# Queries and keys of heads 1 to 4 by seven products of halves with 256 moving columns, and head 5's first

## The chip, the cores and the metric

The kernel runs on one core of one Trainium2 chip. The metric is device time in microseconds (us), lower is better. The core has a matrix engine (TensorE, PE in the profile), a vector engine (DVE), a scalar engine (ACT), GpSimd (POOL) and a queue that issues loads (SyncE, SP).

## The reference, cut to what matters

A trunk of two layers over 512 tokens with 2048 features. The first layer is a retention layer of 8 heads; each has 256 columns of queries, 256 of keys, 512 of values and 512 of gates.

```
h = rmsnorm(x, norm_g[0]) * (1.0 + scale) + shift        # (512, 2048)
proj = h @ w_in                                          # w_in: (2048, 12288)
q, k, v, g = split(proj, [2048, 4096, 8192])
y = chunkwise_retention(rope(q), rope(k) * 256**-0.5, v) # per head
x = x + gate * ((silu(g) * groupnorm(y)) @ w_out)
```

The second layer (latent attention, 16 heads) works on the result. `shift`, `scale` and `gate` come from `silu(c) @ ada_w[i] + ada_b[i]`. The change touches `proj` of the first layer: columns of q and k.

## The kernel before

**Three products.** Every f32 factor is split in two `fp32r` parts, a high one (ACT casts, `L137`) and a low one (DVE subtracts the high part from the value, `L138`). A product is three matmuls into one PSUM bank: high by high, high by low, low by high (`mm3`, `L163` to `L165`). `hT[kt]` is h so split: 16 tiles of 128 features x 512 tokens.

**Steps.** The projections are a list `steps`. A step has units (`load` of weights on SP's queue into a raw tile, `prepare`: high and low part), `multiply` (24 matmuls as a rule) and `follow` (what is done with finished banks). The loop at the end of the printed code goes through them: it issues loads until three units beyond the prepared ones are on their way, prepares the units of step i + 1, multiplies step i, then does the modulation adds fetched in the step before (`rows`: one row is a load of 512 KB and a DVE instruction with an accumulator, `L913`, "mod"; they form the next modulations from `ada_w`), the sums of h if the step has them, and `follow`. `behind` and `queued` tie what is issued to the last instruction of the engines named, so that the blocks stand on their engines' queues in this order; inside of a block a scheduler orders. A queue is worked in order.

**Queries and keys** (`qk_steps`, a head's columns are 512: q and k). Eight steps of two feature blocks; the weights are stationary (128 x 128), h moves with all 512 tokens; four PSUM banks (`acc`). ACT copies the banks out (`keep_rows`, `L641`) and POOL stores them to `qk_d`.

**Values and gates** (`seven_steps`) of one head form a product of 2 x 2 halves with seven products for eight: halves of the tokens, of the features (odd and even blocks), and of the columns (values, gates). DVE forms sums of the weights' halves (`L786` to `L800`); sums of the halves of h lie ready in `sums1` (`form_sums`, 8 pieces u, each two feature blocks). A head is two sweeps of eight steps: the first with four products (24 matmuls of 512 columns a step), the second with three (18). Banks are called x, s, z, y; m1, m4, m5 are copies of them. At the end (`finish`) ACT copies x (values) and applies silu to s, DVE forms `m4` and `m5` (`L850`, `L852`), ACT applies silu to m5 (`L853`), POOL stores. In the names, `vg3_01e` is head 3, first sweep, unit 1, even block; `_r`, `_h`, `_l` are raw tile, high and low part.

**Order before:** q/k of head 1 and 2 (`form_sums` spread over their steps), values/gates of 1 and 2, then q/k and values/gates of 3, of 4 and of 5, then values/gates of 6 and 7; q/k of heads 6 and 7 follow in the next phase, the retention itself from about 960 us on. Head 0 is done ahead of this list.

**Buffers.** Raw tiles: two tags of three each, in turns. Parts: four sets in turns (`own` one, `whi`/`wlo` three). PSUM: `acc` 4 banks and `aux` 4. In the second layer the product `uv` has 256 moving columns.

## Time and profile before

| | |
|---|---|
| median of 3 runs | 2178.03 us (2175.65 to 2179.16) |
| profiled execution | 2178.51 us, span 2176.7 us, granted clock 0.998 |
| PE | 2150.4 us busy, 99% of the span, 10206 matmuls |
| weight loads (PEld) | 1798.4 us, 83% |
| DVE / ACT / POOL | 1563.9 us (72%) / 1015.1 us (47%) / 100.4 us (5%) |
| DMA | 440.26 MB, mean 202 GB/s |

One core, one program: a row of the timeline is start, duration, engine, line, operation, output<-inputs, with a bracket [idle time before it <- what ended it]. A row of groups by line has a count, then busy time and mean ns, then idle time before and what ended it. PE's idle time is what counts where PE is busy 99% of the span.

### The profile page before, as it was taken

Reading aid. Unit: us, or ns where it says so; the run is one execution under the profiler, and the core shown is the slowest. Engines: PE = TensorE matmul, PEld = TensorE weight load, DVE = VectorE, ACT = ScalarE, POOL = GpSimd, SP = SyncE. Lnnn points to the kernel's source line nnn. Section 1 sums busy time; section 2 is a strip of 40 time slices with the busy share of each in tenths; the row PEclk is TensorE's granted clock in tenths of the full one; section 3 lists DMA queues with packets and bytes.
Section 4 is the critical chain, followed back from the end, with each engine's and each line's share of the span. In section 5 each row is a group of like instructions: output and inputs, shape, how many; then the busy total and the mean of one; then the engine's idle time right before and its main releaser. Section 6 shows DMA issues by size and latency. Waiting matters only on the chain.

```text
span 2176.7 us, 27707 instructions
## 1 busy us (share of the span) xinstructions
PE 2150.4 (99%) x10206; PEld 1798.4 (83%) x10206; DVE 1563.9 (72%) x2311; ACT 1015.1 (47%) x1549; POOL 100.4 (5%) x175
## 2 busy tenths in 40 slices
PE   8999999999999999999999999999999999999997
PEld 6888888888888877888888888898888889888887
DVE  8987878676776789656776777667977677775545
ACT  6763344344343454434344445344444365664443
POOL 0000000000000000000000000010000000000000
PEclk9999999999999999999999999999999999999999
DMA  9966767857667778564646465453458723335333
GB/s 387 377 243 199 244 225 231 293 181 268 217 234 251 238 232 296 192 218 152 234 157 220 151 216 185 146 174 107 160 188 314 247 88 100 89 109 183 111 101 133
DMA packets 204971, 440.26 MB, mean 202 GB/s; under 512 B 19313, under 2 KB 56209, under 8 KB 200993
## 3 DMA queue, kind: packets, MB, share of 16 engines
q1 hardware_dynamic: 192768, 399.57, 55.4%
q0 software_dynamic: 11920, 38.91, 4.6%
q8 instruction: 80, 1.31, 0.2%
q14 instruction: 57, 0.47, 0.1%
q10 hardware_dynamic: 146, 0.01, 0.0%
HBM read 395.42 MB, written 43.00 MB: 201 GB/s over the span
## 4 chain that ended last, share of the span: by engine, by line
PE 85%; DVE 7%; issue 4%; ACT 3%; DMA 1%; POOL 0%; DVEq 0%; POOLq 0%; ACTq 0%; SPq 0%
PE o L1211 13%; PE qk L163 4%; PE qk L165 4%; PE qk L164 4%; PE o L2073 4%; PE x L759 2%; PE y L759 2%; PE y L760 2%; PE y L758 2%; PE x L760 2%; PE s L759 2%; PE s L760 2%; PE x L758 2%; PE s L758 2%; PE o L164 2%
## 5 line engine op out<-in xcount | busy, mean ns | idle before, releaser
L1211 PE MATMUL o<-o_h,o_whi 128*128 128x512 f32 (+1 forms) x496 | 192.2, 388 | 0.0
L1211 PE MATMUL o<-o_h,o_wlo 128*128 128x512 f32 (+1 forms) x496 | 191.4, 386 | 0.0
L1211 PE MATMUL o<-o_l,o_whi 128*128 128x512 f32 (+1 forms) x496 | 191.3, 386 | 0.0
L163 PE MATMUL qk<-hT,qk_h 128*128 128x512 f32 x448 | 174.6, 390 | 1.0 <-ACT qk_st L641 1.0
L164 PE MATMUL qk<-hT,qk_h 128*128 128x512 f32 x448 | 174.4, 389 | 0.0
L165 PE MATMUL qk<-hT,qk_l 128*128 128x512 f32 x448 | 174.2, 389 | 0.0
L138 DVE TENSOR_TENSOR o_wlo<-o_r,o_whi 128x1024 fp32r<-128x1024 f32 x61 | 74.6, 1223 | 80.1 <-ACT o_whi L137 80.1
L138 DVE TENSOR_TENSOR qk_l<-qk_r,qk_h 128x1024 fp32r<-128x1024 f32 x56 | 68.1, 1224 | 71.0 <-ACT qk_h L137 70.8
L1211 PEld LDWEIGHTS o<-o_h,o_wlo 128*128 128x128 f32 x496 | 93.2, 188 | 18.7
L1211 PEld LDWEIGHTS o<-o_l,o_whi 128*128 128x128 f32 x496 | 93.2, 188 | 18.3
L1211 PEld LDWEIGHTS o<-o_h,o_whi 128*128 128x128 f32 x496 | 93.2, 188 | 18.3
L163 PEld LDWEIGHTS qk<-hT,qk_h 128*128 128x128 f32 x448 | 84.1, 188 | 18.8 <-ACT qk_st L641 1.5
L165 PEld LDWEIGHTS qk<-hT,qk_l 128*128 128x128 f32 x448 | 84.1, 188 | 17.5
L164 PEld LDWEIGHTS qk<-hT,qk_h 128*128 128x128 f32 x448 | 84.1, 188 | 17.5
L163 PE MATMUL g<-h,g_h 128*128 128x512 f32 x232 | 90.6, 390 | 0.3 <-ACT g_h L137 0.3
L164 PE MATMUL g<-h,g_h 128*128 128x512 f32 x232 | 90.3, 389 | 0.0
L165 PE MATMUL g<-h,g_l 128*128 128x512 f32 x232 | 89.8, 389 | 0.0
L913 DVE SCALAR_TENSOR_TENSOR mod<-mod,c_bm 128x1024 f32<-128x1024 f32 x64 | 78.1, 1220 | 15.3 <-DMA mod<-in_ada_t_dram 15.3
L137 ACT CAST qk_h<-qk_r 128x1024 fp32r<-128x1024 f32 x56 | 57.8, 1052 | 65.7 <-PE qk L164 54.3
L137 ACT CAST o_whi<-o_r 128x1024 fp32r<-128x1024 f32 x61 | 63.5, 1053 | 19.5 <-issue 10.0
L353 DVE SCALAR_TENSOR_TENSOR aw<-aw,c_all 128x2048 f32<-128x2048 f32 x30 | 67.5, 2286 | 0.0
L138 DVE TENSOR_TENSOR o_w_lo<-o_w_raw,o_w_hi 128x1024 fp32r<-128x1024 f32 x32 | 39.0, 1221 | 37.4 <-ACT o_w_hi L137 37.4
(1264 smaller groups left out, 5995.3 us busy)
## 6 DMA issues: line engine op xcount, KB each, us to landing
mod<-in_ada_t_dram SPq DMA_DIRECT2D x128, 512.0 KB, 5.9
o_r<-in_ret_w_out_dram SPq DMA_DIRECT2D x64, 512.0 KB, 4.2
aw<-in_ada_t_dram SPq DMA_DIRECT2D x30, 1024.0 KB, 7.6
qk_r<-in_ret_w_in_dram SPq DMA_DIRECT2D x112, 256.0 KB, 3.9
g_r<-in_mla_w_in_dram SPq DMA_DIRECT2D x32, 512.0 KB, 4.3
o_w_raw<-in_mla_w_out_dram SPq DMA_DIRECT2D x32, 512.0 KB, 3.7
qk_d<-qk_st POOLq DMA_DIRECT2D x32, 256.0 KB, 3.4
qk_r<-qk_d SPq DMA_DIRECT2D x32, 256.0 KB, 6.1
```

The costliest lines, as they stand in the source:

```text
L137: ACT.copy(hi, src)
L138: DVE.tensor_sub(lo, src, hi.bitcast(F32))
L163: PE.matmul(o, lhs[0], rhs[0], start=first and not seeded, stop=False, skip_group_check=seeded)
L164: PE.matmul(o, lhs[0], rhs[1], start=False, stop=False, skip_group_check=seeded)
L165: return PE.matmul(o, lhs[1], rhs[0], start=False, stop=last, skip_group_check=seeded)
L353: DVE.scalar_tensor_tensor(out=aw, in0=aw, scalar=1.0, in1=c_all, op0=ALU.mult, op1=ALU.mult, accum_out=col,)
L758: PE.matmul(banks[b], a[0], w[0], start=first, stop=False, skip_group_check=True)
L759: PE.matmul(banks[b], a[0], w[1], start=False, stop=False, skip_group_check=True)
L760: PE.matmul(banks[b], a[1], w[0], start=False, stop=True, skip_group_check=True)
L913: DVE.scalar_tensor_tensor(out=aw, in0=aw, scalar=1.0, in1=silu_c[j], op0=ALU.mult, op1=ALU.mult, accum_out=mc[:, j, b : b + 1],)
L1211: PE.matmul(o, w[i][:, ki, c0 + b * P : c0 + (b + 1) * P], a[j], start=first and i + j == 0, stop=last and i == 1, skip_group_check=True,)
L2073: PE.matmul(banks2[b][:, cols], w[0][i][:, 0, b * P : (b + 1) * P], o2_moving(w, u, cols)[j], start=u + i + j == 0, stop=u == KD - 1 and i ...
```

## The change

Q and k of heads 1 to 4 are now formed by seven products too (`narrow_steps`), in another division: halves of the columns (q and k, 256 each), of the features (even and odd blocks) and of the tokens (256 each). The sums of the weights' halves are stationary, the halves (or sums) of h move with 256 tokens. All seven banks `m1` to `m7` are held through the one sweep of 14 steps of 24 matmuls with 256 columns. Per quarter of the features a unit `b11` (four blocks of q), and twice a group of `o` (odd blocks of q and k), `a` (even block of k, then three sums on DVE in place) and `b` (no load; what is left in o's raw tile). The banks are joined by ACT copies and eight DVE adds (`after_o`, `after_a`, `after_b`), and stored by four POOL DMAs (`keep`).

Q and k of head 5 come first, plain, with one piece of the sums of h in each of its eight steps; whole h is formed again on ACT (`again`) and not added from its parts on DVE. The order is then q/k and values/gates of 1, of 2, of 3, of 4, then values/gates of 5, 6 and 7. The modulation rows leave the q/k steps in part: steps 0, 2, 3, 6 of a narrow head have one each, and seven of the eight steps of every second sweep (before: four in heads 1 to 4). Step 11 of a narrow head looks two units ahead with loads, not three.

```diff
@@ -653,17 +653,27 @@
             return base.tile(shape, F32R, tag="k4b", bufs=4, name=f"sums_{n}")
         return more(shape, f"sums_{n}")
-    def form_sums(u, acts, sums, staged, more):
+    def sum_slot(n, more):
+        return sums_tile((n - 8) % KD, more)
+    def again(f, kt):
+        k1 = slice(kt, kt + 1)
+        ACT.activation(f, xT[kt // 2][:, kt % 2, :], AF.Identity, bias=b_col[0][:, k1], scale=a_col[0][:, k1])
+    def added(f, kt):
+        DVE.tensor_add(f, h2[kt][:, 0, :].bitcast(F32), h2[kt][:, 1, :].bitcast(F32))
+    def form_sums(u, whole_h, sums, staged, more, slot):
         e, o = (tmp(f"h_{2 * u + i}_f") for i in range(2))
         for f, kt in ((e, 2 * u), (o, 2 * u + 1)):
-            DVE.tensor_add(f, acts[kt][:, 0, :].bitcast(F32), acts[kt][:, 1, :].bitcast(F32))
+            whole_h(f, kt)
...
-            s = sums[2 * u + i] = sums_tile(2 * u + i, more)
+            s = sums[2 * u + i] = slot(2 * u + i, more)
             split(f[i], s[:, :, 0, :], s[:, :, 1, :])
...
-    wvg = w_ret_in[:, 4096:12288].rearrange("k (j n) -> k j n", j=2)
+    def form_half(acts, sums, n, u):
+        if isinstance(n, tuple):
+            kt, half = n
+            return tuple(acts[2 * u + kt][:, a, half * H : (half + 1) * H] for a in range(2))
+        s = sums[2 * u + (n - 1) // 2]
+        return tuple(s[:, (n - 1) % 2, a, :] for a in range(2))
...
-            self.rows, self.sums = rows, sums
+            self.rows, self.sums, self.ahead = rows, sums, 3
             self.beside = {"load": [], "form": [], "multiply": []}
...
@@ -836,6 +852,125 @@
+    def narrow_steps(name, half_of, form, raw_tile, part_tiles, keep):
+        m = [None] * 8
+        put = {}
+        def bank(i):
+            m[i] = (aux if i in (1, 5, 7) else acc)(f"{name}_m{i}")
+        def product(i, n, u, w, first):
+            f = form(n, u)
+            for b in range(2):
+                o, (hi, lo) = m[i][:, b * H : (b + 1) * H], (a[:, b * P : (b + 1) * P] for a in w)
+                for k, (p, q) in enumerate(((hi, f[0]), (hi, f[1]), (lo, f[0]))):
+                    PE.matmul(o, p, q, start=first and b + k == 0, stop=k == 2, skip_group_check=True)
+        def parts(src, shape, n):
+            hi, lo = part_tiles(shape, n)
+            ACT.copy(hi, src)
+            return (hi, lo), lambda: DVE.tensor_sub(lo, src, hi.bitcast(F32))
+        def quarter(g):
+            b11 = {}
+            def step(load, prepare, forms, u0, nu, follow=None):
+                w = {}
+                def ready():
+                    w["p"] = prepare()
+                def multiply():
+                    for i, n, j in forms:
+                        if u0 == 0:
+                            bank(i)
+                        for u in range(nu):
+                            product(i, n, u0 + u, tuple(t[:, u, :] if j is None else t[:, j, u, :] for t in w["p"]), u0 + u == 0)
+                return Step(load, ready, multiply, follow)
...
+            res = [step(load_b11, prepare_b11, [(1, (0, 0), None)], 4 * g, 4)]
+            for s in range(2):
+                res += pair(g, s, step, b11)
+            return res
+        def pair(g, s, step, b11):
+            u0, t, shape = 4 * g + 2 * s, {}, [P, 2, 2, H]
+            last = u0 == KD // 2 - 2
...
+            def prepare_a():
+                a, o, b = t["a"], t["o"], b11["r"][:, 2 * s : 2 * s + 2]
+                DVE.tensor_sub(o[:, 1], o[:, 1], a[:, 0])
+                DVE.tensor_sub(a[:, 0], a[:, 0], b)
+                DVE.tensor_add(a[:, 1], o[:, 1], b)
+                hl, low = parts(a, shape, f"{name}_a{u0}")
+                DVE.tensor_sub(o[:, 0], o[:, 0], a[:, 1])
+                low()
+                return hl
...
+            def after_o():
+                put["1"] = tmp(f"{name}_p1")
+                ACT.copy(put["1"], m[1])
+                c11 = tmp(f"{name}_c11")
+                DVE.tensor_add(c11, m[2], put["1"])
+                keep(0, 0, c11)
+            def after_a():
+                p1, p5, v = put["1"], tmp(f"{name}_p5"), tmp(f"{name}_v")
+                ACT.copy(p5, m[5])
+                DVE.tensor_add(p1, m[6], p1)
+                DVE.tensor_add(v, p1, p5)
+                DVE.tensor_add(v, m[3], v)
+                keep(0, 1, v)
+                put["5"] = p5
+            def after_b():
+                p1, p5 = put["1"], put["5"]
+                DVE.tensor_add(p1, m[7], p1)
+                DVE.tensor_add(p5, p1, p5)
+                keep(1, 1, p5)
+                DVE.tensor_add(p1, m[4], p1)
+                keep(1, 0, p1)
+            return [
+                step(load_o, prepare_o, [(2, (1, 0), 0), (3, 4, 1)], u0, 2, after_o if last else None),
+                step(load_a, prepare_a, [(5, 1, 0), (6, 2, 1)], u0, 2, after_a if last else None),
+                step(lambda: None, prepare_b, [(7, 3, 1), (4, (1, 1), 0)], u0, 2, after_b if last else None),
+            ]
+        return quarter(0) + quarter(1)
...
-            lambda second, u: int(second and (u % 2 == 1 or (h > 4 and u > 0))),
+            lambda second, u: int(second and u > 0),
         )
     sums1, sums2 = {}, {}
@@ -885,11 +1020,33 @@
...
-    steps = qk_steps(1, sums=lambda u: {1: 0, 2: 1, 4: 2, 5: 3, 6: 4}.get(u))
-    steps += qk_steps(2, rows=lambda u: 1, sums=lambda u: {0: 5, 2: 6, 4: 7}.get(u))
+    def narrow_qk(h):
...
+        def keep(half, j, c):
+            r0 = (4 * h + 2 * j) * P
+            POOL.dma_start(
+                qk_d[r0 : r0 + 2 * P, half * H : (half + 1) * H].rearrange("(b p) t -> p b t", p=P),
+                c.rearrange("p (b t) -> p b t", b=2),
+            )
+        return narrow_steps(
+            f"qk{h}", lambda e, j, u0, n: qk_w[j][e][:, u0 : u0 + n, :], lambda n, u: form_half(hT, sums1, n, u),
+            *turns1, keep,
+        )
+    steps = qk_steps(5, sums=lambda u: u)
     for h in range(1, RH):
-        if 2 < h < 6:
-            steps += qk_steps(h, rows=lambda u: 1)
+        if h < 5:
+            block = narrow_qk(h)
+            for i in (0, 2, 3, 6):
+                block[i].rows = 1
+            block[11].ahead = 2
+            steps += block
         steps += heads_steps(h)
@@ -1550,7 +1707,7 @@
         return l2_tile("pt", 4, name, shape, F32R)
     for u, step in enumerate((ga[5], ga[7], g1[0], g1[2], g1[3], g1[5], g1[6], g1[7])):
-        step.beside["form"].append(lambda u=u: form_sums(u, h2, sums2, staged2, more2))
+        step.beside["form"].append(lambda u=u: form_sums(u, added, sums2, staged2, more2, sums_tile))
     latent = {}
@@ -1940,7 +2097,7 @@
             l2 = tc.tile_pool(name="l2", bufs=1)
             pools["l2"] = l2.__enter__()
         with behind(S_):
-            while n_loaded < min(n_prepared + 3, len(loads)):
+            while n_loaded < min(n_prepared + step.ahead, len(loads)):
                 loads[n_loaded]()
                 n_loaded += 1
             if i in (n_p, n_l2):
@@ -1964,7 +2121,7 @@
                 add()
             fetched = []
             if step.sums is not None:
-                form_sums(step.sums, hT, sums1, staged1, more1)
+                form_sums(step.sums, again, sums1, staged1, more1, sum_slot)
         if i + 1 < len(steps):
             for _ in range(steps[i + 1].rows):
                 with behind(S_):
```

On ACT, at the change from a head's gates to the next q/k. Before (gates of head 2, q/k of head 3; `qk3_0`, `qk3_1` are the first units, `v2_st`, `g2_st` the evictions, `m5` the silu of the last gates):

```order
L137 CAST qk3_0_h_3274<-qk3_0_r_3208 128x1024
L641 ACTIVATE v2_st0_3303<-x2_0_2726 128x512
L641 ACTIVATE v2_st1_3306<-x2_1_2727 128x512
L641 ACTIVATE g2_st0_3309<-s2_0_2728 128x512
L641 ACTIVATE g2_st1_3312<-s2_1_2729 128x512
L853 ACTIVATE m5_2_0_3035<-m5_2_0_3035 128x512
L853 ACTIVATE m5_2_1_3037<-m5_2_1_3037 128x512
L137 CAST qk3_1_h_3328<-qk3_1_r_3239 128x1024
L137 CAST qk3_2_h_3366<-qk3_2_r_3271 128x1024
```

After (gates of head 1, q/k of head 2; `b11`, `o0`, `a0`, `b0` are the first four steps' units):

```order
L872 CAST qk2_b11_0_h_2843<-qk2_b11_0_r_2776 128x1024
L641 ACTIVATE v1_st0_2868<-x1_0_2288 128x512
L641 ACTIVATE v1_st1_2871<-x1_1_2289 128x512
L641 ACTIVATE g1_st0_2874<-s1_0_2290 128x512
L641 ACTIVATE g1_st1_2877<-s1_1_2291 128x512
L988 ACTIVATE m5_1_0_2597<-m5_1_0_2597 128x512
L988 ACTIVATE m5_1_1_2599<-m5_1_1_2599 128x512
L872 CAST qk2_o0_h_2890<-qk2_o0_r_2808 128x1024
L872 CAST qk2_a0_h_2926<-qk2_a0_r_2841 128x1024
L872 CAST qk2_b0_h_2961<-qk2_o0_r_2808 128x1024
```

The cast of the second unit stands behind the same eviction and silu as before, and the third and fourth unit's behind it; the fourth casts from o's raw tile.

On DVE, at the same place. Before:

```order
L850 TENSOR_TENSOR m4_2_0_3074<-m4_2_0_3074,y2_0_2732 128x512
L852 TENSOR_TENSOR m5_2_0_3035<-m5_2_0_3035,y2_0_2732 128x512
L850 TENSOR_TENSOR m4_2_1_3076<-m4_2_1_3076,y2_1_2733 128x512
L852 TENSOR_TENSOR m5_2_1_3037<-m5_2_1_3037,y2_1_2733 128x512
L138 TENSOR_TENSOR qk3_1_l_3329<-qk3_1_r_3239,qk3_1_h_3328 128x1024
L913 SCALAR_TENSOR_TENSOR mod_0_2_1_00_3301,mod_0_2_1_c_3300<-mod_0_2_1_00_3301,c_bm0_1733 128x1024
L138 TENSOR_TENSOR qk3_2_l_3367<-qk3_2_r_3271,qk3_2_h_3366 128x1024
L913 SCALAR_TENSOR_TENSOR mod_0_2_1_01_3361,mod_0_2_1_c_3300<-mod_0_2_1_01_3361,c_bm1_1734 128x1024
L138 TENSOR_TENSOR qk3_3_l_3401<-qk3_3_r_3325,qk3_3_h_3400 128x1024
```

After:

```order
L985 TENSOR_TENSOR m4_1_0_2636<-m4_1_0_2636,y1_0_2294 128x512
L987 TENSOR_TENSOR m5_1_0_2597<-m5_1_0_2597,y1_0_2294 128x512
L985 TENSOR_TENSOR m4_1_1_2638<-m4_1_1_2638,y1_1_2295 128x512
L987 TENSOR_TENSOR m5_1_1_2599<-m5_1_1_2599,y1_1_2295 128x512
L873 TENSOR_TENSOR qk2_o0_l_2891<-qk2_o0_r_2808,qk2_o0_h_2890 128x1024
L1070 SCALAR_TENSOR_TENSOR mod_0_2_0_51_2866,mod_0_2_0_c_1780<-mod_0_2_0_51_2866,c_bm1_1777 128x1024
L929 TENSOR_TENSOR qk2_o0_r_2808<-qk2_o0_r_2808,qk2_a0_r_2841 128x512
L930 TENSOR_TENSOR qk2_a0_r_2841<-qk2_a0_r_2841,qk2_b11_0_r_2776 128x512
L931 TENSOR_TENSOR qk2_a0_r_2841<-qk2_o0_r_2808,qk2_b11_0_r_2776 128x512
L933 TENSOR_TENSOR qk2_o0_r_2808<-qk2_o0_r_2808,qk2_a0_r_2841 128x512
L873 TENSOR_TENSOR qk2_a0_l_2927<-qk2_a0_r_2841,qk2_a0_h_2926 128x1024
L873 TENSOR_TENSOR qk2_b0_l_2962<-qk2_o0_r_2808,qk2_b0_h_2961 128x1024
```

Between the low parts of the second and the third unit stand now four sums (`L929` to `L933`) as well as the modulation add.

On DVE, from q/k to the first sweep of values and gates. Before (end of q/k of head 3; the banks are emptied by ACT):

```order
L138 TENSOR_TENSOR qk3_7_l_3539<-qk3_7_r_3465,qk3_7_h_3538 128x1024
L913 SCALAR_TENSOR_TENSOR mod_0_2_1_30_3532,mod_0_2_1_c_3300<-mod_0_2_1_30_3532,c_bm0_1733 128x1024
L786 TENSOR_TENSOR vg3_00e_r_3499<-vg3_00e_r_3499 128x512
L788 TENSOR_TENSOR vg3_00o_r_3500<-vg3_00o_r_3500,vg3_00e_r_3499 128x512
L789 TENSOR_TENSOR vg3_00o_r_3500<-vg3_00o_r_3500 128x512
L790 TENSOR_TENSOR vg3_00e_l_3574<-vg3_00e_r_3499,vg3_00e_h_3573 128x1024
L793 TENSOR_TENSOR vg3_00o_l_3581<-vg3_00o_r_3500,vg3_00o_h_3580 128x1024
L913 SCALAR_TENSOR_TENSOR mod_0_2_1_31_3567,mod_0_2_1_c_3300<-mod_0_2_1_31_3567,c_bm1_1734 128x1024
L786 TENSOR_TENSOR vg3_01e_r_3534<-vg3_01e_r_3534 128x512
```

After (end of q/k of head 2; `c11`, `v`, `p1`, `p5` are what is stored):

```order
L946 TENSOR_TENSOR qk2_c11_3278<-qk2_m2_2931,qk2_p1_3276 128x512
L873 TENSOR_TENSOR qk2_b6_l_3290<-qk2_o6_r_3151,qk2_b6_h_3289 128x1024
L952 TENSOR_TENSOR qk2_p1_3276<-qk2_m6_2978,qk2_p1_3276 128x512
L953 TENSOR_TENSOR qk2_v_3318<-qk2_p1_3276,qk2_p5_3317 128x512
L954 TENSOR_TENSOR qk2_v_3318<-qk2_m3_2944,qk2_v_3318 128x512
L802 TENSOR_TENSOR vg2_00e_r_3281<-vg2_00e_r_3281 128x512
L804 TENSOR_TENSOR vg2_00o_r_3282<-vg2_00o_r_3282,vg2_00e_r_3281 128x512
L805 TENSOR_TENSOR vg2_00o_r_3282<-vg2_00o_r_3282 128x512
L806 TENSOR_TENSOR vg2_00e_l_3329<-vg2_00e_r_3281,vg2_00e_h_3328 128x1024
L809 TENSOR_TENSOR vg2_00o_l_3336<-vg2_00o_r_3282,vg2_00o_h_3335 128x1024
L960 TENSOR_TENSOR qk2_p1_3276<-qk2_m7_2998,qk2_p1_3276 128x512
L961 TENSOR_TENSOR qk2_p5_3317<-qk2_p1_3276,qk2_p5_3317 128x512
```

The adds from the banks m6 and m3 stand ahead of the first unit of values and gates (`vg2_00`), those from m7 and m4 behind it and ahead of `vg2_01`.

On PE, the first matmuls of the second step at the first place. Before (second unit of q/k of head 3; `L163` to `L165` are the three products):

```order
L163 MATMUL qk3_0_3332<-hT_2_388,qk3_1_h_3328 128x512
L164 MATMUL qk3_0_3332<-hT_2_388,qk3_1_h_3328 128x512
L165 MATMUL qk3_0_3332<-hT_2_388,qk3_1_l_3329 128x512
L163 MATMUL qk3_1_3333<-hT_2_388,qk3_1_h_3328 128x512
L164 MATMUL qk3_1_3333<-hT_2_388,qk3_1_h_3328 128x512
L165 MATMUL qk3_1_3333<-hT_2_388,qk3_1_l_3329 128x512
L163 MATMUL qk3_2_3334<-hT_2_388,qk3_1_h_3328 128x512
```

After (step `o0` of head 2):

```order
L868 MATMUL qk2_m2_2931<-hT_1_318,qk2_o0_h_2890 128x256 x2
L868 MATMUL qk2_m3_2944<-sums_9_1453,qk2_o0_h_2890 128x256 x2
L868 MATMUL qk2_m2_2931<-hT_1_318,qk2_o0_l_2891 128x256
L868 MATMUL qk2_m2_2931<-hT_1_318,qk2_o0_h_2890 128x256 x2
L868 MATMUL qk2_m2_2931<-hT_1_318,qk2_o0_l_2891 128x256
L868 MATMUL qk2_m2_2931<-hT_3_403,qk2_o0_h_2890 128x256 x2
L868 MATMUL qk2_m2_2931<-hT_3_403,qk2_o0_l_2891 128x256
L868 MATMUL qk2_m2_2931<-hT_3_403,qk2_o0_h_2890 128x256 x2
```

The weights' part is the stationary tile in both. Ahead of the first matmul with the low part (`o0_l`) stand four with the high one, for two banks, where two for one bank stood before.

## The prediction

> **What bounds the kernel now.** First the page's parts 1 and 4, then the waits of PE, then stretches of the stage that is changed.

> ```profile
> PE 2150.4 (99%) x10206; PEld 1798.4 (83%) x10206; DVE 1563.9 (72%) x2311; ACT 1015.1 (47%) x1549; POOL 100.4 (5%) x175
> PE 85%; DVE 7%; issue 4%; ACT 3%; DMA 1%; POOL 0%; DVEq 0%; POOLq 0%; ACTq 0%; SPq 0%
> ...
> PE qk L163 <- ACT qk_st L641: 1.0, 1, 1.0
> PE x L759 <- DVE vg_01e_l L790: 1.0, 2, 0.5
> PE x L759 <- DVE vg_17o_l L800: 0.6, 1, 0.6
> ```

> TensorE (PE) is the bound: the three waits are all that it waits from 160 to 900 us. Fewer PE cycles there come out as time, and so does every new wait of PE. The stretches (us, then busy time of PE, weight loads, DVE, ACT, POOL, the granted clock, DMA share, GB/s) are q and k of head 3, the first and second sweep of its values and gates, the second sweep of head 5, head 6's two, and the second sweep of head 7:

> ```profile
> 402.49:446.06 43.57, 43.57 (x194) 36.04 (x192) 26.00 (x35) 12.33 (x14) 3.77 (x8) 1.00 0.84 284
> 446.06:490.11 44.05, 44.05 (x194) 36.06 (x192) 33.72 (x40) 19.73 (x22) 0.81 (x2) 1.00 0.65 204
> 490.11:523.24 33.13, 33.13 (x145) 27.03 (x144) 23.41 (x32) 15.42 (x21) 1.91 (x4) 1.00 0.66 213
> 731.61:765.57 33.96, 33.40 (x145) 26.95 (x144) 28.00 (x39) 15.01 (x21) 0.13 (x1) 1.00 0.83 281
> 765.57:810.75 45.18, 44.66 (x194) 35.91 (x193) 39.49 (x49) 21.67 (x26) 4.17 (x8) 1.00 0.76 243
> 810.75:844.19 33.44, 33.39 (x145) 26.96 (x144) 28.00 (x39) 14.99 (x21) 0.13 (x1) 1.00 0.85 284
> ...
> 889.42:922.56 33.14, 33.14 (x146) 27.04 (x145) 21.46 (x30) 15.42 (x21) 1.93 (x4) 1.00 0.56 178
> ```

> q and k of one head are 192 matmuls with 512 columns in 43.57 us: one each 0.2269 us.

> **The matmuls.** Four heads go from 192 such matmuls to 7×8×2×3 = 336 with 256 columns and a new weight block each. The same shape runs today in the second layer; its first and last of 30 in a row, with its weight load:

> ```profile
> 1806.08 0.28 PE L164 MATMUL uv<-ukv,kvT 128*128 128x256 f32 x1
> ...
> 1809.55 0.28 PE L163 MATMUL uv<-ukv,kvT 128*128 128x256 f32 x1
> ...
> L164 PEld LDWEIGHTS uv<-ukv,kvT x128: 187/192/192, 1744.4 to 1970.2; 128*128 128x128 f32 x128
> ```

> 3.47 us over 29 steps is 0.1197 us. A narrow head is 336×0.1197 = 40.2 us, 3.35 less than 43.57; four heads give back 13.4 us. The ends of this price are half of the wide one (0.1135 us, 21.7 us back) and the row itself; I take the row. [...]

> **The start of a narrow head.** A step was 24 wide matmuls, 5.44 us; it is 24 narrow ones, 2.87 us. What ACT and DVE must do between two steps does not halve. The same place in the run before is the change from head 2's gates to head 3's q and k (PE crosses at E = 402.49):

> ```profile
> 402.61 0.68 DVE L852 TENSOR_TENSOR m<-m,y 128x512 f32<-128x512 f32 x1
> 403.21 0.68 DVE L850 TENSOR_TENSOR m<-m,y 128x512 f32<-128x512 f32 x1
> 403.80 0.68 DVE L852 TENSOR_TENSOR m<-m,y 128x512 f32<-128x512 f32 x1
> 406.12 1.23 DVE L138 TENSOR_TENSOR qk_l<-qk_r,qk_h 128x1024 fp32r<-128x1024 f32 x1 [1.64 <-ACT qk_h L137]
> 407.26 1.22 DVE L913 SCALAR_TENSOR_TENSOR mod<-mod,c_bm 128x1024 f32<-128x1024 f32 x1
> 408.41 0.08 DVE L913 DVE_READ_ACCUMULATOR mod<-mod,c_bm 128x1 f32 x1
> ...
> 404.52 0.63 ACT L853 ACTIVATE m<-m 128x512 f32<-128x512 f32 x1 [0.56 <-DVE m L852]
> 405.06 1.98 ACT L137 CAST qk_h<-qk_r 128x1024 fp32r<-128x1024 f32 x2
> ...
> L137 ACT CAST qk_h<-qk_r 128x1024 fp32r<-128x1024 f32 x56 | 57.8, 1052 | 65.7 <-PE qk L164 54.3
> ```

> The second unit's high part is cast behind the last gate's silu, from E+2.57 to E+3.6, and its low part ends at 407.35, E+4.86. Before, PE needed them at E+5.44. Now the same places in the queues hold qk_o, and PE needs it at E+2.87. In the order PE does four matmuls of the high part first (0.48): it starts at 3.65, waits for the low part until 4.90, has 20 left (2.39) and ends the step at 7.30 instead of 5.74. Late: 1.6.

> The next step is dearer. DVE does, behind qk_o's low part, a modulation add (1.15 by the rows), then three dependent subtractions; ACT casts; DVE forms the low part. Subtractions of this size and the form with an accumulator bank:

> ```profile
> 444.72 0.69 DVE L788 TENSOR_TENSOR vg_01o_r<-vg_01o_r,vg_01e_r 128x512 f32<-128x512 f32 x1
> 445.45 0.69 DVE L789 TENSOR_TENSOR vg_01o_r<-vg_01o_r 128x512 f32<-128x512 f32 x1
> 447.82 1.23 DVE L790 TENSOR_TENSOR vg_01e_l<-vg_01e_r,vg_01e_h 128x1024 fp32r<-128x1024 f32 x1 [1.68 <-ACT vg_01e_h L787]
> ...
> 446.26 0.60 ACT L641 ACTIVATE qk_st<-qk 128x512 f32<-128x512 f32 x1 [0.76 <-PE qk L165]
> 446.75 1.04 ACT L787 CAST vg_01e_h<-vg_01e_r 128x1024 fp32r<-128x1024 f32 x1
> ...
> L826 DVE TENSOR_TENSOR y<-y,m 128x512 f32<-128x512 f32 x14 | 9.7, 700 | 5.2 <-PE y L760 5.2
> ```

> A dependent subtraction starts 0.73 after the one before, a free one 0.60 (402.61 to 403.80). So: add E+4.77 to 5.92, subtractions at 5.92, 6.64, 7.24, cast 7.97 to 9.02, low part to 10.27. PE ends that step at 10.32 + 2.39 = 12.71 instead of 8.61: 4.1 late in all. The second pair repeats it with DVE still behind: low part at 19.1, PE wants it at 18.9, 4.3 in all. From there a quarter (seven steps) is 20.1 us for PE, and for DVE seven low parts of 1.14, eight subtractions of 0.66, two modulation adds of 1.15 and two waits of 0.5 for a cast, 16.6, so the rest is in time.

> Head 1 comes behind q and k of head 5, without gates to finish: by the fence above its cast can run at E+0.69 (446.75 against E = 446.06), the low part ends at E+3.0 and costs nothing; the subtraction step ends at 8.45 + 2.39 = 10.84, 2.2 late, 2.5 with the second pair. Sum at the starts: 3×4.3 + 2.5 = 15.4 us. Unseen here is whether the subtractions' operands land; loads are issued three units ahead and q/k loads land in 3.9 us, so I set that at nothing (ends: nothing, and the 1.9 us that a late load cost once, below).

> ```profile
> qk_r<-in_ret_w_in_dram SPq DMA_DIRECT2D x112, 256.0 KB, 3.9
> ```

> **The end of a narrow head.** The banks are now emptied by DVE. Its queue holds three adds that wait for the last matmul of step 13 (F; visible 0.2 later, as 446.26 against 446.06), and behind them the first unit of values and gates: adds at F+0.2, 0.92, 1.64 (0.70 each), subtraction 2.26, cast 2.98 to 4.03, low part to 5.53, second cast to 5.48, its low part to 6.67, then three more adds to 8.62. PE arrives at F+2.87, gets the first high part at 4.08, the second at 5.53, does six and eight matmuls to 8.93, finds the bank of s_1 free, ends at 10.30 instead of 8.31. The next unit's cast ends at 10.31 and its second at 11.76: 0.6 more. So 2.6 us a head, 10.4 in all. Before, ACT emptied these banks, and the stretch 446.06:490.11 is only 0.5 over its 192 matmuls. The ends of this term: 0.1 if the high parts were ready at F+2.87, 4.0 if PE had to take the matmuls in the plain order, each low part behind its high one.

> **Small terms.** Second sweeps of heads 1 to 4 take seven modulation adds instead of four: 33.96, 33.44 and 33.14 with seven against 33.13 with four, 0.4 each, 1.5 in all. Head 5's first sweep now follows head 4's second: 45.18 against 44.05, 1.1. All sums of h in one block of eight steps: per step ACT has a cast 1.0, two activations of 0.80 as below, a wait of 1.3 for three small DVE operations, two casts of 0.6, 5.1 of 5.44 us; only the first is late, behind the eight evictions of head 0, 0.4 (ends 0 and 2).

> ```profile
> L247 ACT ACTIVATE h_2f<-x,b_col,a_col x1: 801/801/801, 44.0 to 44.0; 128x512 f32<-128x512 f32 x1
> ...
> 169.92 0.42 DVE L661 TENSOR_TENSOR sums_f<-h_f 128x256 f32<-128x256 f32 x1
> ...
> L137 ACT CAST sums<-sums_f x4: 616/618/620, 170.8 to 177.1; 128x512 fp32r<-128x512 f32 x4
> ```

> Nothing for the rest: the same 4 MB of weights a head in 14 issues for 16; four stores a head as before, read only after 960 us; 16 adds less on DVE, 16 activations more on ACT, under PE's block.

> **Sum.** −13.4 + 15.4 + 10.4 + 1.5 + 1.1 + 0.4 = +15.4. The profiled run's own time is 2178.5 (span 2176.7), 0.5 above the median of the runs; it gives 2193.9, and I say 2194.

> **Rivals.**
> *Faster.* DVE and ACT run ahead, so the subtraction steps and the first units of values and gates are there in time; only the 1.6 behind the gates' silu stays, at three heads. 2178.5 − 13.4 + 4.7 + 1.5 = 2171. For it: four sets of parts let them prepare three units ahead, and DVE has 3.5 us free in each quarter. Against: their queues are in order, and the rows at 404.52 and 405.06 show the cast stuck behind the silu. It decides when all waits of a narrow head stay under 2.4 us.
> *Even.* The chains are half as long, the waits 13 us: 2181.
> *A late modulation load on top.* With seven adds a sweep DVE has stood still for a load:

> ```profile
> 759.10 1.23 DVE L913 SCALAR_TENSOR_TENSOR mod<-mod,c_bm 128x1024 f32<-128x1024 f32 x1 [1.87 <-DMA mod<-in_ada_t_dram]
> ```

> Once or twice at each of the four starts, in a chain with no slack: 7 to 15 us more, 2201 to 2209. Against: in the new order the loads stand farther ahead.
> *Weight loads show.* If a load could not run under the matmul before it, a narrow matmul would cost its 0.188 us or more: 4×(63.2 − 43.6) = 78 us, 2257. The uv rows at 0.12 us with a load of 0.19 each speak against it. [...]

> **How the numbers follow.** About 0.2% (4.4 us) is what a measurement of this kernel tells from no change. Forecast, 2186 to 2204: 0.58. Late loads: 0.14. Faster: 0.17. Even: 0.09. Weight loads: 0.01; something else 0.01. A range of 2174 to 2207 takes in the even case and the upper edge of the faster one; it leaves out most of the faster one, 0.14, the upper part of the late one, 0.04, and the last two. Faster by over 0.2% 0.17, within 0.07 (most of the even case), slower 0.76.

> **What would show it.** PE of narrow heads spaced at 0.12; 2 to 5 us of PE waits for qk_o_l and qk_a_l at the start of heads 2 to 4, less at head 1; waits for vg_00e, vg_00o and vg_01 behind each narrow head; DVE idle for PE at the three adds. I am wrong if PE passes these places without a wait, or if a narrow head takes under 42 us.

## The result, and the profile after

The changed kernel took 2198.64 us (median of 4, 2196.72 to 2201.54) against 2178.55: slower by 20.1 us, ratio 1.0096 with a 95% interval of 1.0079 to 1.0113. The forecast was 2194, in a range of 2174 to 2207. The profiled execution is the longest of the four, 2201.54 us, its span 23.1 us longer than before.

From the page, the busy times:

```profile
PE 2152.1 (98%) x10782; PEld 1821.0 (83%) x10782; DVE 1641.4 (75%) x2411; ACT 1043.8 (47%) x1581; POOL 103.9 (5%) x175
```

The longest waits of PE from 160 to 1000 us (sum, times, longest):

```profile
PE qk_m L868 <- ACT qk_a_h L872: 5.9, 4, 1.5
PE x L774 <- ACT vg_00e_h L803: 4.6, 4, 1.1
PE qk_m L868 <- DVE qk_a_l L873: 2.1, 4, 0.5
PE z L774 <- ACT vg_00o_h L808: 2.0, 4, 0.5
PE qk_m L868 <- ACT qk_o_h L872: 1.9, 3, 0.6
PE qk_m L868 <- DVE qk_o_l L873: 1.6, 3, 0.5
PE x L775 <- DVE vg_01e_l L806: 1.5, 3, 0.5
```

The waits stand where the prediction put them: qk_o at three heads, qk_a at four, vg_00 behind all four. The stretches (length, then busy time of PE, weight loads, DVE, ACT, POOL, the granted clock, DMA share, GB/s) are q/k of head 1, its two sweeps, the same three of head 2, and the first sweep of head 3:

```profile
204.20:249.45 45.25, 42.32 (x338) 41.71 (x336) 34.90 (x44) 15.63 (x17) 2.27 (x4) 0.96 0.52 162
249.45:295.31 45.86, 45.02 (x192) 35.92 (x193) 40.17 (x48) 20.37 (x22) 1.43 (x2) 1.00 0.66 209
295.31:328.38 33.07, 33.07 (x145) 27.03 (x144) 26.70 (x38) 15.22 (x21) 1.53 (x3) 1.00 0.81 270
328.38:375.64 47.26, 42.90 (x338) 41.88 (x336) 36.90 (x48) 16.31 (x18) 4.24 (x8) 0.96 0.62 199
375.64:421.63 45.99, 45.17 (x192) 35.90 (x193) 40.24 (x48) 20.39 (x22) 1.43 (x2) 1.00 0.65 207
421.63:454.74 33.11, 33.11 (x145) 27.03 (x144) 27.17 (x40) 15.32 (x21) 1.65 (x3) 1.00 0.82 272
501.89:548.42 46.53, 46.03 (x193) 37.29 (x193) 40.18 (x48) 20.36 (x22) 1.44 (x2) 0.96 0.66 206
```

A narrow head is 45.3 to 47.3 us, where the plain one was 43.57. Its stretch ends with PE's first matmul of values and gates and so holds the 1.3 us gap ahead of that matmul as well. What the prediction did not have is in the column of the clock: 0.96 where before it was 1.00. In each such stretch the granted clock drops to 0.50 for one window of 3.41 us; this is called a fall here. The rows are: two windows before it in head 2, the fall, and the window behind; then two windows at the ends of heads 2 and 3 (one without, one with a fall behind it):

```profile
332.71:336.12 3.41, 2.73 (x21) 2.45 (x20) 3.38 (x6) 0.00 (x0) 0.00 (x0) 1.00 1.05 417
336.12:339.53 3.41, 1.50 (x10) 1.30 (x11) 2.94 (x4) 2.94 (x3) 0.00 (x0) 1.00 0.94 338
339.53:342.95 3.42, 3.42 (x18) 3.42 (x18) 3.42 (x5) 0.00 (x0) 0.00 (x0) 0.50 0.86 233
342.95:346.36 3.41, 3.41 (x31) 3.41 (x30) 2.91 (x6) 1.04 (x2) 0.00 (x0) 1.00 0.50 181
373.67:377.08 3.41, 1.80 (x10) 1.11 (x9) 3.32 (x6) 2.09 (x2) 0.73 (x1) 1.00 0.22 77
499.96:503.37 3.41, 1.78 (x11) 1.10 (x9) 3.32 (x6) 2.09 (x2) 0.73 (x1) 1.00 0.22 77
503.37:506.79 3.42, 3.42 (x8) 2.74 (x9) 3.28 (x5) 0.00 (x0) 0.61 (x1) 0.50 0.63 178
```

PE was busy for less than half of the window 336.12:339.53, in its waits for qk_a; in the next it does 18 matmuls where it otherwise does 31, at clock 0.50. Five such falls lie ahead of 600 us, at the starts of all four narrow heads and at the end of head 3's.

The start of head 2 in the timeline (ACT, then DVE; E = 328.38) is the chain of the prediction, row by row:

```profile
330.42 0.63 ACT L988 ACTIVATE m<-m 128x512 f32<-128x512 f32 x1 [0.56 <-DVE m L987]
330.96 1.03 ACT L872 CAST qk_o_h<-qk_o_r 128x1024 fp32r<-128x1024 f32 x1
336.41 1.04 ACT L872 CAST qk_a_h<-qk_a_r 128x1024 fp32r<-128x1024 f32 x1 [4.42 <-DVE qk_a_r L931]
...
332.02 1.23 DVE L873 TENSOR_TENSOR qk_o_l<-qk_o_r,qk_o_h 128x1024 fp32r<-128x1024 f32 x1 [1.63 <-ACT qk_o_h L872]
333.16 1.22 DVE L1070 SCALAR_TENSOR_TENSOR mod<-mod,c_bm 128x1024 f32<-128x1024 f32 x1
...
335.63 0.68 DVE L931 TENSOR_TENSOR qk_a_r<-qk_o_r,qk_b_r 128x512 f32<-128x512 f32 x1
...
337.49 1.23 DVE L873 TENSOR_TENSOR qk_a_l<-qk_a_r,qk_a_h 128x1024 fp32r<-128x1024 f32 x1 [0.44 <-ACT qk_a_h L872]
```

The cast of qk_o stands behind the silu and begins at E+2.58; the cast of qk_a waits 4.42 us for the last of the three sums, which stand behind qk_o's low part and the modulation add; qk_a's low part ends at E+10.3, where the prediction had 10.27.

### The profile page after: what moved, and what is told of

It is laid out like the page before. It is cut to its first block, busy times and chain, and to the rows that moved or that the text cites. A ratio compares the mean times of both kernels' runs of the same rounds, so it can differ in the third digit from the quotient of the medians.

```text
span 2199.8 us, 29029 instructions
## 1 busy us (share of the span) xinstructions
PE 2152.1 (98%) x10782; PEld 1821.0 (83%) x10782; DVE 1641.4 (75%) x2411; ACT 1043.8 (47%) x1581; POOL 103.9 (5%) x175
## 4 chain that ended last, share of the span: by engine, by line
PE 79%; DVE 10%; issue 5%; ACT 3%; DMA 2%; POOL 0%; DVEq 0%; ACTq 0%; SPq 0%; POOLq 0%
PE o L1368 13%; PE qk_m L868 6%; PE o L2230 4%; PE x L775 2%; PE qk L163 2%; PE qk L165 2%; PE qk L164 2%; PE x L776 2%; PE y L775 2%; PE y L776 2%; PE y L774 2%; PE s L775 2%; PE s L776 2%; PE g L163 2%; PE g L164 2%
## 5 line engine op out<-in xcount | busy, mean ns | idle before, releaser
L138 DVE TENSOR_TENSOR o_wlo<-o_r,o_whi 128x1024 fp32r<-128x1024 f32 x61 | 74.6, 1223 | 80.5 <-ACT o_whi L137 80.5
L163 PE MATMUL g<-h,g_h 128*128 128x512 f32 x232 | 90.6, 390 | 0.3 <-ACT g_h L137 0.3
L164 PE MATMUL g<-h,g_h 128*128 128x512 f32 x232 | 90.3, 389 | 0.0
L165 PE MATMUL g<-h,g_l 128*128 128x512 f32 x232 | 89.8, 389 | 0.0
L163 PE MATMUL qk<-hT,qk_h 128*128 128x512 f32 x192 | 75.0, 391 | 1.1 <-ACT qk_st L641 1.1
L164 PE MATMUL qk<-hT,qk_h 128*128 128x512 f32 x192 | 74.7, 389 | 0.0
L165 PE MATMUL qk<-hT,qk_l 128*128 128x512 f32 x192 | 74.6, 389 | 0.0
L137 ACT CAST o_whi<-o_r 128x1024 fp32r<-128x1024 f32 x61 | 63.5, 1052 | 19.9 <-issue 10.0
L138 DVE TENSOR_TENSOR o_w_lo<-o_w_raw,o_w_hi 128x1024 fp32r<-128x1024 f32 x32 | 39.0, 1221 | 37.3 <-ACT o_w_hi L137 37.3
L138 DVE TENSOR_TENSOR o_l<-o_in,o_h 128x1024 fp32r<-128x1024 f32 x24 | 29.4, 1223 | 48.7 <-ACT o_h L137 48.7
L868 PE MATMUL qk_m<-sums,qk_a_h 128*128 128x256 f32 x256 | 51.3, 303 | 5.9 <-ACT qk_a_h L872 5.9
L2230 PE MATMUL o<-o_l,o_w_hi 128*128 128x512 f32 (+1 forms) x160 | 55.5, 347 | 0.9 <-DVE o_l L138 0.9
L2230 PE MATMUL o<-o_h,o_w_hi 128*128 128x512 f32 (+1 forms) x160 | 55.7, 348 | 0.2 <-ACT o_h L137 0.2
L2230 PE MATMUL o<-o_h,o_w_lo 128*128 128x512 f32 (+1 forms) x160 | 55.4, 346 | 0.0
## 6 DMA issues: line engine op xcount, KB each, us to landing
qk_r<-in_ret_w_in_dram SPq DMA_DIRECT2D x48, 256.0 KB, 3.3
qk_o_r<-in_ret_w_in_dram SPq DMA_DIRECT2D x32, 256.0 KB, 3.8
qk_r<-qk_d SPq DMA_DIRECT2D x32, 256.0 KB, 5.9
```

The source lines that it names most:

```text
L137: ACT.copy(hi, src)
L138: DVE.tensor_sub(lo, src, hi.bitcast(F32))
L163: PE.matmul(o, lhs[0], rhs[0], start=first and not seeded, stop=False, skip_group_check=seeded)
L164: PE.matmul(o, lhs[0], rhs[1], start=False, stop=False, skip_group_check=seeded)
L165: return PE.matmul(o, lhs[1], rhs[0], start=False, stop=last, skip_group_check=seeded)
L868: PE.matmul(o, p, q, start=first and b + k == 0, stop=k == 2, skip_group_check=True)
```

## The experiments

The ratios are to runs of the kernel before that were taken beside each group; their medians are 2178.55, 2178.2 and 2177.86 us, so a difference between an experiment and the changed kernel (2198.64) is good to about 0.7 us.

**The order without the narrow form.** Head 5's q and k first with all sums, plain q and k in heads 1 to 4:

```diff
-            block = narrow_qk(h)
...
-            steps += block
+            steps += qk_steps(h, rows=lambda u: int(u % 2 == 0))
```

> The changed kernel's order with the plain form: head 5's q and k first with all sums of h, then q and k of heads 1 to 4 as before (192 matmuls of 512 columns, one modulation row at every second step), each ahead of its values and gates; seven rows in every second sweep. It leaves the narrow form out alone. By the changed kernel's trace the order costs 0.1 (sums) + 0.6 (second sweeps) + 1.2 (head 5's first sweep) less 0.4 (second sweeps of 5 and 6): 2179 to 2181; the prediction's terms say 2181.5. Rival (the order itself is what costs): 2185 or more.

It took 2179.68 us against 2177.86, ratio 1.0009 (1.0000 to 1.0018). The order costs about 1.8 us (0 to 4 by the interval), as expected; the narrow form as it was built costs the other 18.

**The starts.** `reach` says how many steps ahead the loop prepares:

```diff
             def prepare_o():
                 hl, low = parts(t["o"], shape, f"{name}_o{u0}")
                 low()
+                if u0 == 0:
+                    sums_a()
                 return hl
...
+            block[0].ahead = 2
+            steps[-1].reach = 2
             steps += block
...
-        n_prepared += prepare_for(i + 1)
+        while n_ready <= i + step.reach:
+            n_prepared += prepare_for(n_ready)
+            n_ready += 1
```

> Only the starts of the four narrow heads are changed: the second unit (qk_o) and the three sums for the third are done on ACT and DVE ahead of what finishes the gates (or q/k of head 5), not behind it. In the changed kernel's trace the four narrow heads hold 20.4 us more than 4 x 336 matmuls at 0.12 us, up to their last matmul (3.6 at head 1, 5.6, 5.5 and 5.6 at heads 2 to 4). Theory (the units stand in the queue behind the silu and the adds, and the granted clock of 0.50 in the 3.4 us after is a consequence of PE's waits): nearly all of it goes, the clock stays at 1.00 at these places, 17 to 20 us less, 2179 to 2182. Rival (DVE has too much to do, the wait only moves on to the low parts behind): half or less goes, 2188 or more. Rival (the clock falls for another reason than the waits): about 14 us go and the clock still falls.

It took 2191.0 us, only 7.6 less than the changed kernel: the theory's 17 to 20 were a miss, the rival that the wait moves on was right. PE's waits for qk_o went (3.5 us) and the clock fell at one start instead of four (1.00 in the stretches of heads 2 and 3, 0.996 over the execution against 0.994); the waits for qk_a stayed at 8.0 us in all (4.2 for the high part and 3.8 for the low one; in the changed kernel 5.9 and 2.1), though the sums were done early. In the profiled executions the gain is 8.0 us (spans 2191.8 and 2199.8), and three falls fewer, at 1.2 us each (next experiment), are 3.6 of it.

**The ends.** The first unit of values and gates is prepared ahead of the adds that empty the banks:

```diff
             block[11].ahead = 2
+            block[12].reach = 2
+            block[13].ahead = 2
```

> Only the ends of the narrow heads are changed: the first unit of values and gates (vg_00) is prepared ahead of the adds that empty the banks behind step 12 and 13. In the changed kernel's trace the ends hold 13.4 us: 1.3 us before the first matmul of each of the four heads, and 8.2 us in their first sweeps against 4 x 44.05. Theory: 10 to 13 of them go, 2186 to 2189. Rival (the next unit, vg_01, comes late instead, since the three last adds and its own sums now are all that is between): 4 to 6 us go, 2193 to 2195.

It took 2186.72 us, 11.9 less, as the theory said. In the profiled executions it is 14.9 (spans 2184.9 and 2199.8): 10.4 at the ends, and the rest at the starts, where four falls are gone. Head 2's q/k and first sweep, by stretches:

```profile
325.31:370.06 44.75, 41.49 (x337) 40.47 (x336) 37.92 (x48) 17.05 (x19) 3.51 (x7) 1.00 0.66 211
370.06:414.94 44.88, 44.81 (x195) 35.87 (x193) 39.01 (x48) 19.36 (x21) 2.15 (x3) 1.00 0.66 211
```

The first sweep is 44.88 instead of 45.99, and the gap of 1.3 in front of it is gone. The starts were not touched here, and yet head 2's is shorter: 44.75 is 1.2 less than 47.26 - 1.3, with the clock at 1.00 throughout. The same waits stand in the four starts (5.9 us in all for qk_a_h, 2.1 for qk_a_l, 1.8 and 1.6 for qk_o). So one fall of the clock at a start costs 1.2 us, and in this execution there was none (granted clock 0.998 over all of it, as before the change). One more execution of the changed kernel (the first below) agrees: head 3's stretch took 45.98 us without a fall, where it took 47.15 above with one.

**Both.**

> Both of the two edits before. Theory: the waits are what the narrow form costs, and without them its shorter matmuls (4 x 3.3 us) are left: 2178.5 - 13 + 1 to 4 us for the new order = 2166 to 2170, faster than the kernel before. Rival (what goes at one end comes back at the other): 2175 to 2185.

It took 2180.56 us, 18 less than the changed kernel but still 1.0010 (1.0001 to 1.0019) of the one before. The theory's 2166 to 2170 were a miss. The time is in the rival's range, though not for its reason: nothing came back at the ends (first sweeps of 44.9 us). What is left is at the starts. Head 3 begins at 444.99; DVE and then ACT:

```profile
445.34 1.22 DVE L1081 SCALAR_TENSOR_TENSOR mod<-mod,c_bm 128x1024 f32<-128x1024 f32 x1
446.48 0.68 DVE L992 TENSOR_TENSOR m<-m,y 128x512 f32<-128x512 f32 x1
...
448.28 0.68 DVE L994 TENSOR_TENSOR m<-m,y 128x512 f32<-128x512 f32 x1
448.88 1.22 DVE L1081 SCALAR_TENSOR_TENSOR mod<-mod,c_bm 128x1024 f32<-128x1024 f32 x1
...
450.62 1.22 DVE L873 TENSOR_TENSOR qk_a_l<-qk_a_r,qk_a_h 128x1024 fp32r<-128x1024 f32 x1
...
448.99 0.63 ACT L995 ACTIVATE m<-m 128x512 f32<-128x512 f32 x1 [0.56 <-DVE m L994]
449.53 1.03 ACT L872 CAST qk_a_h<-qk_a_r 128x1024 fp32r<-128x1024 f32 x1
```

The sums were moved ahead of the gates' adds, and so pushed these back: with a modulation add in front, they begin 1.5 us behind E (444.99), where in the changed kernel, at head 2, they began 0.5 ahead of it. The silu and the cast of qk_a_h wait for them, and a second modulation add stands ahead of qk_a_l.

**Modulation rows later,** in the changed kernel, without the other edits:

```diff
-            for i in (0, 2, 3, 6):
+            for i in (6, 7, 8, 9):
                 block[i].rows = 1
```

> The changed kernel with the four modulation rows of a narrow head at steps 6, 7, 8 and 9, not at 0, 2, 3 and 6; nothing else. Theory (DVE's queue sets the start): the add between qk_o's low part and the three sums (1.15 us) goes, so the third unit comes 1.1 us earlier at four heads, 4.6 us, and where PE idles less the clock falls less often (1.6 us each, up to four): 4 to 10 us less, 2189 to 2195. Rival (ACT's cast behind the silu and the chain of sums set it, the add fits beside): under 2 us.

It took 2190.6 us, 8.0 less: the theory's. The waits for qk_a_h fell from 5.9 to 1.9 us, about one modulation add at each of four heads; in head 2's stretch the clock stayed at 1.00 (44.74 us), and over the execution it was 0.997 against 0.994. This one line gives as much as the longer edit of the starts.

**All three:** both edits, and no modulation add on DVE from the end of a head to step 5 of the next.

```diff
-            lambda second, u: int(second and u > 0),
+            lambda second, u: int((0 < u < 7 if second else u == 5) if h < 4 else second and u > 0),
...
-            for i in (0, 2, 3, 6):
+            for i in (6, 7, 8, 9):
```

> The kernel with both edits (starts and ends), and with no modulation add in DVE's queue from the last step of a head's second sweep to step 5 of the next narrow head: rows at steps 6 to 9 of it, at steps 1 to 6 of the second sweeps of heads 1 to 3, and one at step 5 of their first sweeps. Both edits alone left 12.1 us over 4 x 336 matmuls at 0.12 us in q and k, in waits for qk_a behind the adds. Theory (DVE's queue at the start): 8 to 12 of them go, 2169 to 2173, 0.2 to 0.4% faster than before. Rival (they come back in the second quarter or in values and gates, DVE being full): 2176 to 2181.

It took 2170.1 us against 2177.86, ratio 0.9964 (0.9952 to 0.9977): faster than both kernels, and in the theory's range. Q and k of heads 2 and 3 and the first sweep of head 2, by stretches:

```profile
322.70:363.73 41.03, 40.51 (x337) 40.30 (x336) 36.73 (x47) 16.32 (x19) 4.46 (x8) 1.00 0.69 229
363.73:408.56 44.83, 44.77 (x194) 35.82 (x193) 40.48 (x52) 19.38 (x21) 2.16 (x3) 1.00 0.70 223
441.67:481.80 40.13, 40.13 (x337) 40.12 (x336) 35.57 (x45) 16.23 (x18) 3.41 (x6) 1.00 0.70 228
```

The waits of PE that are left from 160 to 940 us:

```profile
PE x L775 <- DVE vg_01e_l L806: 1.5, 3, 0.5
PE qk_m L868 <- DVE qk_a_l L873: 1.0, 2, 0.5
PE qk L163 <- ACT qk_st L641: 0.9, 1, 0.9
```

Head 3 takes 40.13 us without a wait, 0.1194 a matmul; heads 2 and 4 have one wait for qk_a_l each and take 41.03. So 40.13 is the narrow form's own price, 3.4 us below the plain one.

**Filling PE's idle time,** in the changed kernel, with a weight tile of the step before (`spare`):

```diff
...
+                            for _ in range(({5: 16} if name == "qk1" else {2: 12, 5: 20}).get(i, 0)):
+                                PE.matmul(
+                                    m[i][:, :H], spare["w"], hT[0][:, 0, :H], start=True, stop=True, skip_group_check=True
+                                )
...
```

> The changed kernel with idle PE time filled: 12 matmuls of 256 columns ahead of step o and 20 ahead of step a of the first group in heads 2 to 4, 16 ahead of step a in head 1, into the bank that the step then starts anew; their results are not used. They take about as long as PE waits there, so the waits stay and only PE is busy meanwhile. Theory (the granted clock falls to 0.50 for 3.4 us because PE idled through most of the 3.4 us before): no fall at these four places, 1.6 us less each, 5 to 7 us in all, 2192 to 2194. Rival (the clock falls for the load that DVE, ACT and the transfers make there, or for the narrow matmuls): it still falls, no change or up to 2 us slower.

It took 2195.37 us, 3.3 less and so short of the theory's 2192 to 2194; in the profiled executions it is 5.9 (spans 2193.9 and 2199.8). Head 2's stretch:

```profile
327.44:373.51 46.07, 44.89 (x369) 44.16 (x367) 36.79 (x48) 16.18 (x18) 4.25 (x8) 1.00 0.63 203
```

PE does 32 matmuls more and is done 1.2 us earlier than in 47.26, at clock 1.00, as in head 3's stretch (46.04). This does not hang on how the windows happen to lie, as it may with changed ends: here PE is busy for 44.89 of the 46.07 us, and its list of waits has none for qk_o or qk_a any more. DVE, ACT and the transfers have the same work as before (36.79, 16.18, 203 GB/s against 36.90, 16.31, 199). So the falls at these starts came with PE's idle time, not with the narrow matmuls and not with the load on DVE and ACT. The gain was overstated: 1.6 us was counted for a fall, and it is 1.2.

**The changed kernel again,** for the places of the falls.

> The changed kernel once more, one profiled execution. In its first trace the clock fell to 0.50 five times for 3.41 us before 600 us, at starts that lie whole multiples of 3.413 us apart, and the span was 2199.8 us. The same waits stood in the kernel with changed ends, where it did not fall at the starts at all. Theory (windows of 3.413 us on a grid that does not start with the kernel; the clock falls behind a window in which PE was busy for about 0.36 or less): the waits of PE come out the same, the number of falls n differs, and the span is 2199.8 - 1.6 x (5 - n). Rival (the falls belong to places of the kernel): five falls at the same places.

> As the run before: a third execution of the changed kernel, for the number of falls of the clock and the span.

> As the two runs before: a fourth execution of the changed kernel.

The waits came out the same in all (5.9, 4.6, 2.1, 2.0 us for the first four). The falls did not: 3, 5 and 5 ahead of 650 us (granted clock 0.996, 0.993 and 0.994 over the executions), in part at other places, so the rival is out. The theory's 0.36 was an estimate that no run bears out by the profile's busy time: in the first profile falls came behind windows with PE busy for 1.35 to 1.78 us, 0.40 to 0.52 of 3.41. The spans were 2196.6, 2198.1 and 2198.7 against 2199.8. The theory's formula gives 2196.6 for three falls, as measured, but 2199.8 for five, where two executions are 1.1 and 1.7 us shorter: the span follows the number only in part. Most of the rest lies in sweeps without a fall: in the second of the three runs head 4's second sweep took 33.26 us and head 7's first 44.44, where the first profile has 33.89 and 45.23. From the first of these, the window with qk_a's waits in head 3 (no fall behind it), the one at head 3's end (none), and the one at head 4's end (a fall):

```profile
460.78:464.19 3.41, 1.82 (x13) 1.41 (x12) 2.90 (x5) 1.88 (x2) 0.00 (x0) 1.00 0.93 328
498.32:501.74 3.42, 1.80 (x10) 1.11 (x9) 3.33 (x6) 2.10 (x2) 0.73 (x1) 1.00 0.22 77
624.62:628.03 3.41, 1.78 (x11) 1.10 (x9) 3.32 (x6) 2.09 (x2) 0.73 (x1) 1.00 0.22 77
```

## Why the prediction was right, and where it was off

The time was in the range and the direction right, for the reason given: the steps became half as long and the chains between two steps did not. The terms, in the profiled execution, the longest of the four (us):

| term | forecast | measured | from |
|---|---|---|---|
| 4 x 336 narrow matmuls | -13.4 | -13.8 | 4 x (40.13 - 43.57) |
| starts, heads 2 to 4 | 4.3 each | 4.6 each | 44.75 - 40.13, with changed ends, no fall |
| start, head 1 | 2.5 | 2.6 | 45.25 - 40.13 - 1.3 - 1.2 (a fall) |
| ends, four heads | 10.4 | 12.7 | 4 x 1.3, and first sweeps 8.1 longer, less one fall 0.6 |
| falls of the clock | none | 5.4 | 4 x 1.2 at starts, 0.6 at an end |
| modulation, head 5, sums | 3.0 | 1.5 | +0.6, +1.2, +0.1, and 0.4 less in sweeps of heads 5 and 6 |
| all else | 0 | 0.8 | 0.4 less ahead of 154 us, 1.2 more behind 944 us |
| sum | 15.4 | 23.0 | spans 2199.8 and 2176.7 (23.1 as rounded) |

The starts were right to a third of a microsecond a head, with their instructions: the cast behind the silu, the sums behind the modulation add. At head 2 PE begins qk_o at E+3.66, gets its low part at 4.92 and qk_a's at 10.39, where the prediction had 3.65, 4.90 and 10.32. The 0.2 us of the second group show where no fall slowed PE ahead of it (head 3 of the first run again: the low part at E+19.27, forecast 19.1); behind a fall that wait does not come (head 2: PE waits for nothing from 344 to 352 us).

The ends were mis-sized by 0.6 us a head. The first high part came 1.3 us late (1.2 forecast), but behind it the second high part and the unit vg_01 took 1.9 more in place of 1.4.

The term that was missing is the clock. The prediction took a wait of PE at its own length; here a cluster of waits is followed by 3.41 us at half clock, at four of four starts in the profiled execution. With the ends it is most of why this execution took 7.6 us more than the 2193.9 of the sum; the median is 4.7 above it.

Seven modulation adds in the second sweep were put at 0.4 a head by rows of heads 5 to 7; three of the four heads had none of it (33.07 and 33.11 us), only head 4's sweep was 0.75 longer.

The rivals. Faster: its mechanism, DVE and ACT in time at these places, did not happen here, and for the most part does in the kernel with all three edits, at 2170.1 where the rival said 2171. That the numbers meet is in part luck: the rival's sum holds 4.7 us behind the silu, which that kernel does not have, and that kernel's first sweeps of heads 1 to 4 are still 2.9 us longer than before. Even and late modulation loads: the waits were not half as long, none of PE's rows leads to a load, and DVE waits for none at the four starts. Weight loads show: 40.13 us for 336 matmuls with as many weight loads leave no room for it, where a load lasts 0.19 us and 336 of them one behind another would be over 63. For the price of a narrow matmul the row (0.1197) was right: 0.1194 was measured.

## What to carry to other kernels

A form with fewer PE cycles in more and shorter steps is worth what the engines that prepare can deliver at the seams: write down the queue of ACT and DVE there and count how far ahead of PE they stand. Look first for work in that queue that nobody waits for (the modulation adds gave 8.0 us by one line), then for preparation that can go ahead of what waits for PE. At the ends that gave 11.9 us by itself; at the starts, where the queue was full, it pushed other work back and gave 7.6. And waits of PE that added up to 1.8 to 2.1 us of a window of 3.41 cost more than their length at the starts here, by 1.2 us for each fall of the clock.

## What the runs showed of the hardware

```profile
328.31:331.72 3.41, 1.93 (x14) 1.53 (x13) 3.36 (x5) 3.15 (x4) 1.31 (x3) 1.00 0.92 329
570.65:574.06 3.41, 1.93 (x15) 1.53 (x14) 3.36 (x6) 2.64 (x4) 1.60 (x3) 1.00 0.87 290
```

What a fall costs is 1.2 us at a start, where a part of it covers a wait that would come anyway (0.2 us of the second group), and 0.6 at an end (46.53 against 45.86 to 45.99).

The longest wait of PE that the changed kernel's profile lists is 1.5 us. In its windows it is the sum of the gaps that tells the falls apart (1.63 us and more of 3.41 with a fall behind, 1.61 and less without), not the longest gap: in the kernel with changed ends a wait of 1.6 us stood at a start without a fall.
